# Seven landing buffers for weights become ten, in space taken from GpSimd's DMA descriptors

## The chip, the cores and the metric

The kernel runs on one core of a Trainium2 chip. The metric is device time in microseconds (us) of one execution. TensorE (PE in the profile, its weight loads PEld) multiplies matrices, VectorE (DVE) and ScalarE (ACT) work on elements, GpSimd (POOL) does some element work and issues small transfers, SyncE (SP) issues large transfers. 16 DMA engines carry every transfer, whoever issues it.

## The reference

One inference step of a hybrid model with two layers: 128 context tokens (group 0) and 128 latent tokens (group 1) of width 2048, which share the weights and differ in their modulation.

```
for l in range(2):
    shift1, scale1, gate1, shift2, scale2, gate2 = split(silu(c) @ w_mod[l] + b_mod[l])   # per group
    h = x * (1 + scale1) + shift1
    q, k, v, hq, hff, hfb, hi, hgt = split(h @ w_in[l])            # 2048 x 6656
    att = rms_norm(attention(q, k, v, sink))                       # 8 heads, 2 key/value heads
    hg, s_f, s_b = hgrn(hq, hff, hfb, hi, hgt, lower bounds, states)   # forward and backward scan
    x = layer_norm(alpha * x + gate1 * (concat(att, hg) @ w_o[l]))     # 2048 x 2048
    u = (x * (1 + scale2) + shift2) @ w_up[l]                      # 2048 x 8192
    x = layer_norm(alpha * x + gate2 * (square(relu(u)) @ w_down[l]))  # 8192 x 2048
```

Everything is float32. The outputs are x of both groups, keys and values of the context, and the final scan states.

## The kernel before, in words

All weights come from HBM once. A weight tile is 512 rows by 512 columns, 1 MB, and arrives as two halves of 128 partitions by 1024 floats (0.524 MB, 4 KB in each partition), each in a landing buffer `raw` of the pool `rawp`, which has `RAW_BUFS` = 7 buffers. `split` takes a half apart into a rounded high part `wh` (ScalarE, L1324) and the remainder `wl` (VectorE, L1325), each with a pool of `W_BUFS` = 4 halves. After `wl` the landing buffer is free. `mm_tile` then makes three products for each piece, high by high, high by low, and low by high, into accumulators in PSUM: lines L436, L438, L439 for units whose result is transposed, L448 to L450 for the others. Each unit (512 columns of a matrix) is four such tiles.

The modulation weights `w_mod` go through the same landing buffers. Part of them is multiplied on TensorE straight from the buffer (`Mod`, L203, and `ModQ`, L223, for the first two vectors of layer 0); part of them on VectorE (`ModH`, four L266 steps for each tile, the sum over partitions later on TensorE, L275). They are mixed in among the weight tiles in a list `seq` at set rates: in layer 0's projections 8/13, 16/13 and 1.2 modulation tiles for each weight tile, in layer 0's MLP 0.111 for TensorE and 0.45 for VectorE, in layer 1 far fewer. What a layer norm needs and has not come yet is put right ahead of it (`flush`).

The last part of the program walks through `seq`. `issue` puts the loads of up to 20 items ahead on SP's queue, in the order of `seq`, but stops when as many buffers are taken as `RAW_BUFS` says; `split` splits the current tile and the next weight tile; after every tile a few steps of side work (attention, the scans, modulation, layer norm outputs) are advanced by `pump`. The queues of SP and GpSimd are in the order in which the program writes them. ScalarE, VectorE and TensorE are ordered by the framework's planner, which works with estimated durations and the number of buffers in each pool; the orders are fixed when the kernel is built.

GpSimd issues the small loads (`side`): constants, residual rows `Y` (L1185), gate rows `G` (L876), bias rows, scan states, scale and shift of the layer norms (L951, L952, L998, L999). Descriptors of its transfers are written into a space reserved in each partition of SBUF, 16 KB unless `Bacc` is told otherwise (`dynamic_dma_scratch_size`). ScalarE issues the stores of states, keys and gate rows (`back`). SP and ScalarE write no descriptors into that space.

A unit's results are taken from PSUM by steps such as L1236 (accumulator `Z` of the MLP), L1240 and L1241 (gated sum), L887 to L892 (residual sum), L541 and L511 (softmax), L742 and L748 (scan).

```
                while len(hs) < 2:
                    if live[0] >= RAW_BUFS:
                        return
                    raw = rawp.tile([128, 1024], F32, tag="raw", name=nm("raw"))
                    nc.sync.dma_start(raw, half_src(it, len(hs)))
```

Of the kernel before, what the change touches and what calls it, by code (L numbers as in the profile page):

```python
# [22 lines left out]
SCALE = 128.0 ** -0.5  # L23
LN_EPS = 1e-5
RMS_EPS = 1e-6
RAW_BUFS = 7
W_BUFS = 4
PUMP2 = 2
PUMP = 3
# [16 lines left out]


class Unit:
    """One [2048, 512] block of a weight matrix against the tokens of both groups."""

    def __init__(self, kind, src, act, done, groups=range(4)):
        self.kind = kind
# [9 lines left out]
def tile_hybrid_step(ctx: ExitStack, tc: tile.TileContext, a, o):  # L62
    nc = tc.nc
    PS = bass.MemoryType.PSUM

    const = ctx.enter_context(tc.tile_pool(name="const", bufs=1))
    rawp = ctx.enter_context(tc.tile_pool(name="rawp", bufs=RAW_BUFS))
    whp = ctx.enter_context(tc.tile_pool(name="whp", bufs=W_BUFS))
# [18 lines left out]
    def u(tag, n=512):  # L87
        return up.tile([128, n], F32, tag=tag, name=nm(tag), bufs=BUFS[tag])

    def pair(s):  # L90
        t = actp.tile([128, 1024], F32, tag="a", name=nm(s))
        return [t[:, 0:512], t[:, 512:1024]]

    def small(n, s="s"):
        return sp.tile([128, 16], F32, tag="s", name=nm(s))[:, :n]

    def bank(s="b"):
        return sdp.tile([128, 512], F32, tag="sd", name=nm(s))

    def v3(t, n):  # L100
        return t.rearrange("p (m x) -> p m x", m=n)
# [3 lines left out]
    side = nc.gpsimd  # L105
# [4 lines left out]
        side.dma_start(t, a[name])  # L110
        return t

    # ---- constants and small parameters
    craw = const.tile([128, 16, 2], F32, name="craw")
    nc.sync.dma_start(craw, a["cT"])
    stat = const.tile([128, 16, 2], F32, name="stat")
# [25 lines left out]
    K = {}  # L142
# [37 lines left out]
        dve.tensor_tensor(lb1, m, e0, ALU.subtract)  # L180
        dve.tensor_scalar(oml1, lb1, -1.0, 1.0, ALU.mult, ALU.add)

    # ---- modulation vectors
    modT = {}
    grow = {}

    class Mod:
        """One modulation vector; its four blocks of 512 features lie 32 partitions apart."""

        def __init__(self, l, v):  # L190
            self.l, self.v = l, v
# [13 lines left out]
                          tile_position=(0, 32 * j))  # L205

    class ModQ:
        """512 features of one modulation vector, its products summed over four parts of the rows."""

        def __init__(self, l, v, q):  # L210
            self.l, self.v, self.q = l, v, q
# [33 lines left out]
    dve.memset(ones32, 1.0)  # L245

    class ModH:
        """1024 features of one modulation vector, summed over the rows on the vector engine, over partitions on the PE."""

        def __init__(self, l, v, h):  # L250
            self.l, self.v, self.h = l, v, h
# [103 lines left out]
                dve.tensor_tensor(mtv[:, j], ptv[:, j], bt[:, j], ALU.add)  # L355
        modT[l, v] = mt

    # ---- queue of side work, advanced one stage per weight tile
    tasks = deque()

    def start(gen, banks=0):
# [36 lines left out]
            pump(1)  # L398
        return dct[key]

    # ---- activations, transposed and split in two
    def new_act(s):
        return (actp.tile([128, 4, 256], F32R, tag="a", name=nm(s + "h")),
                actp.tile([128, 4, 256], F32R, tag="a", name=nm(s + "l")))
# [3 lines left out]
        act.copy(hi, src)  # L408
        dve.tensor_tensor(lo, src, hi.bitcast(F32), ALU.subtract)  # L409

    # ---- weight tiles
    class Main:
        def __init__(self, unit, kg):
            self.unit, self.kg = unit, kg
# [35 lines left out]
                        pe.matmul(ps, lhsT=lo[:, k, gs], rhs=wh[k], start=False, stop=e and k == 3)  # L450

    def ev(un, eng0, eng1, where):
        """The two blocks of a finished unit, in SBUF; what earlier parts of its rows gave is added."""
        if un.base is None:
            t = pair("ev") if where == "A" else [u(where), u(where)]
            eng0(t[0], un.ps[0])
            eng1(t[1], un.ps[1])
            return t
        for b in range(2):
            dve.tensor_tensor(un.base[b], un.ps[b], un.base[b], ALU.add)  # L460
        return un.base

    # ---- attention
    kS = {}
    kP = {}
    vP = {}
# [30 lines left out]
        kP[l], kS[l], vP[l], vS[l] = kt, ks, kvp, (kvs, vc)  # L497

    def softmax(l, j, banks_, nk, e):
        """e[t, head, key] = exp(scale * s - m); returns 1 / (sum + exp(K["sink"] - m))."""  # L500
        hb = 4 // len(banks_)
        mx, t, sm, es = small(4), small(4), small(4), small(4)
        for b, ps in enumerate(banks_):
            dve.tensor_reduce(mx[:, hb * b:hb * b + hb], v3(ps, hb), AX.X, ALU.max)
        sk = K["sink"][:, 8 * l + 4 * j:8 * l + 4 * j + 4]
        dve.scalar_tensor_tensor(mx, mx, SCALE, sk, ALU.mult, ALU.max)
        dve.tensor_tensor(es, sk, mx, ALU.subtract)
        dve.tensor_scalar(t, mx, -1.0, None, ALU.mult)
        for h in range(4):
            ps = v3(banks_[h // hb], hb)[:, h % hb]  # L510
            act.activation(e[h], ps, AF.Exp, scale=SCALE, bias=t[:, h:h + 1], accum_out=sm[:, h:h + 1])  # L511
        act.activation(es, es, AF.Exp)
        dve.tensor_tensor(sm, sm, es, ALU.add)
        dve.reciprocal(sm, sm)
        return sm
# [91 lines left out]
            tk[l, "att"] = start(att_fin(l), 1)  # L607

    def rstd_of(v, n, scale, eps):
        """(scale * v + eps) ** -0.5, refined by one Newton step."""  # L610
        x, r, t = small(n), small(n), small(n)
        dve.tensor_scalar(x, v, scale, eps, ALU.mult, ALU.add)
        act.activation(r, x, AF.Ln)
        act.activation(r, r, AF.Exp, scale=-0.5)
        dve.tensor_tensor(t, r, r, ALU.mult)
        dve.tensor_tensor(t, t, x, ALU.mult)
        dve.tensor_scalar(t, t, -0.5, 1.5, ALU.mult, ALU.add)
        dve.tensor_tensor(r, r, t, ALU.mult)
        return r
# [27 lines left out]
                split_act(hls[j], (slice(None), slice(0, 4), slice(128 * g, 128 * g + 128)), v3(t, 4))  # L647
            mix[l, j] = hls[j]

    # ---- HGRN  # L650
    vh = {}
    qh = {}
    oh = {}
# [210 lines left out]
            dve.scalar_tensor_tensor(lo, pt, gcol, hi.bitcast(F32), ALU.mult, ALU.subtract)  # L864
        mix[l, 2 + G] = hl_

    # ---- residual, layer norm
    xres = {}
    yt = {}
    bst = {}  # L870
# [8 lines left out]
    def stats(key, n, g):  # L879
        if n == 0:  # L880
            bst[key, g] = sp.tile([128, 24], F32, tag="bs", name=nm("bs"), bufs=4)
        dve.bn_stats(bst[key, g][:, 6 * n:6 * n + 6], yt[key, n, g])

    def add_gated(key, n, g, ps, gt, first, last):
        """y += gate * ps (y starts as alpha * residual)."""
        t = gt
        dve.tensor_tensor(t, ps, gt, ALU.mult)  # L887
        y = yt[key, n, g]
        if first:
            dve.scalar_tensor_tensor(y, y, ALPHA, t, ALU.mult, ALU.add)  # L890
        else:
            (dve if n == 3 else pool).tensor_tensor(y, y, t, ALU.add)  # L892
        if last:
            stats(key, n, g)

    def ln_stat(key):
        """Mean and 1 / sqrt(variance + eps) of every token, one column a group."""
        mv = small(4)
        for g in range(2):
            dve.bn_aggr(mv[:, 2 * g:2 * g + 2], bst[key, g])  # L900
        r = rstd_of(mv.rearrange("p (g x) -> p g x", g=2)[:, :, 1], 2, 1.0, LN_EPS)
        return [(mv[:, 2 * g:2 * g + 1], r[:, g:g + 1]) for g in range(2)]
# [17 lines left out]
        return A, B  # L920

    def ln_mod(key, AB, dst):
        """h = (xhat * g + b) * (1 + scale) + shift, transposed and split."""
        A, B = AB
        for n in range(4):
            hl = new_act("h")
            for g in range(2):
                y = yt[key, n, g]
                pt = bank("pt")
                for c in range(4):  # L930
                    pe.transpose(pt[:, 128 * c:128 * c + 128], y[:, 128 * c:128 * c + 128], K["ident"])
                t = u("ed")
                if g == 0:
                    dve.tensor_tensor(v3(t, 4), v3(pt, 4),
                                      A[:, 4 * n:4 * n + 4, g:g + 1].to_broadcast([128, 4, 128]), ALU.mult)
                    dve.tensor_tensor(v3(t, 4), v3(t, 4),
                                      B[:, 4 * n:4 * n + 4, g:g + 1].to_broadcast([128, 4, 128]), ALU.add)
                else:
                    for c in range(4):
                        act.activation(t[:, 128 * c:128 * c + 128], pt[:, 128 * c:128 * c + 128], AF.Identity,  # L940
                                       scale=A[:, 4 * n + c, g:g + 1], bias=B[:, 4 * n + c, g:g + 1])
                split_act(hl, (slice(None), slice(0, 4), slice(128 * g, 128 * g + 128)), v3(t, 4))
            dst[n] = hl
# [47 lines left out]
            store(n, g)  # L991

    def ln_out(key, li, sink_fn):
        """x = xhat * g + b, off the critical path."""
        tag = "G"
        for n in range(4):
            gt, bt = u(tag), u(tag)
            side.dma_start(gt, a["lng"][li:li + 1, 512 * n:512 * n + 512].partition_broadcast(128))  # L998
            side.dma_start(bt, a["lnb"][li:li + 1, 512 * n:512 * n + 512].partition_broadcast(128))  # L999
            for g in range(2):  # L1000
                y = yt.pop((key, n, g))
                pool.tensor_tensor(y, y, gt, ALU.mult)
                pool.tensor_tensor(y, y, bt, ALU.add)
                sink_fn(n, g, y)
            yield

    # ---- the program
    modseq = deque()
    poolseq = deque()
    POOLED = ((0, 5), (1, 0), (1, 1), (1, 2), (1, 5))  # L1010
# [271 lines left out]
    for l in range(L):  # L1282
        layer(l)

    # ---- emit
    raws = {}
    live = [0]
    nd = [0]
# [8 lines left out]
    def issue(upto):  # L1297
        while nd[0] < min(upto, len(seq)):
            it = seq[nd[0]]
            if it[0] in ("main", "mod"):  # L1300
                hs = raws.setdefault(nd[0], [])
# [3 lines that stand above are left out]
# [24 lines left out]
            nsplit[0] += 1  # L1329

    def main_ahead(i, n):
        """Index just past the n-th main tile after position i."""
        j = i + 1
        while j < len(seq) and n > 0:
            if seq[j][0] == "main":
                n -= 1
            j += 1
        return j

    for i, it in enumerate(seq):  # L1340
        issue(i + 1 + 20)
        split(i + 1)
        if it[0] == "main":
            split(main_ahead(i, SPLIT_AHEAD))
            issue(i + 1 + 20)
            m = it[1]
# [137 lines left out]
```

## Time and profile before

| | us |
|---|---|
| median of 3 runs | 2680.48 |
| lowest and highest | 2664.18, 2681.79 |
| profiled execution, first to last instruction | 2678.7 |
| TensorE busy in it | 2553.7 (95%) |
| VectorE, ScalarE, GpSimd busy | 1862.2, 1212.4, 226.2 |

The profiled span is 1.8 us below the median. Spans of matmuls overlap and their ends are modelled, so busy time on TensorE says when it had work and not how fast it went. The kernel reads 643.32 MB from HBM and writes 6.88 MB.

### The profile page before, as it was taken

What the parts mean: (1) busy time and instruction counts of PE and PEld (TensorE: products, weight loads), DVE (VectorE), ACT (ScalarE), POOL (GpSimd) and SP (SyncE); (2) the same over time, 40 slices, a digit from 0 to 9 for tenths busy, and PEclk for the clock granted to TensorE, in tenths of its full rate; (3) what the DMA queues carried; (4) which work ended last, traced back from release to release, by engine and by line L of the source; (5) the groups of instructions that cost most, each with busy time, mean ns of one, the idle gap of its engine ahead of it and who ended that gap; (6) DMA issues with size and microseconds to landing.
All of it is one profiled execution on the core that took longest, in us unless ns stands there. A gap on an engine that the chain in (4) does not pass through costs nothing.

```text
span 2678.7 us, 41129 instructions
## 1 busy us (share of the span) xinstructions
PE 2553.7 (95%) x16276; PEld 2189.5 (82%) x16276; DVE 1862.2 (70%) x2290; ACT 1212.4 (45%) x1655; POOL 226.2 (8%) x266
## 2 busy tenths in 40 slices
PE   7999999988999999999998999999899999999996
PEld 4787777656988978979876989898798898998985
DVE  3555777658877868787778777787876556566566
ACT  2434554334444534533533656544454444443442
POOL 2000000014100000000014100000330000000002
PEclk9999999999999999999999999999899999999998
DMA  9879878778887878787778656476666666666664
GB/s 325 272 270 316 279 245 273 264 246 322 276 285 268 276 251 298 267 274 249 260 260 275 238 172 228 149 237 200 200 213 221 208 212 229 203 219 211 212 207 141
DMA packets 192369, 652.91 MB, mean 244 GB/s; under 512 B 22752, under 2 KB 25376, under 8 KB 192176
## 3 DMA queue, kind: packets, MB, share of 16 engines
q1 hardware_dynamic: 177680, 614.56, 67.5%
q0 software_dynamic: 11552, 33.04, 4.2%
q8 instruction: 127, 2.08, 0.3%
q10 hardware_dynamic: 2944, 2.69, 0.3%
q14 instruction: 66, 0.54, 0.1%
HBM read 643.32 MB, written 6.88 MB: 243 GB/s over the span
## 4 chain that ended last, share of the span: by engine, by line
PE 60%; issue 24%; DMA 8%; DVE 6%; ACT 2%; POOL 0%; SPq 0%; DVEq 0%; ACTq 0%; POOLq 0%
PE acc L436 9%; PE acc L438 9%; PE acc L439 9%; PE acc L448 9%; PE acc L449 9%; PE acc L450 9%; DMA raw<-in_w_mod_dram 3%; DMA raw<-in_w_in_dram 2%; PE psm L203 2%; DMA raw<-in_w_o_dram 2%; DVE wl L1325 2%; PE pX L777 1%; ACT wh L1324 1%; PE psm L223 1%; DMA out_nsf_dram<-lf 1%
## 5 line engine op out<-in xcount | busy, mean ns | idle before, releaser
L1324 ACT CAST wh<-raw 128x1024 fp32r<-128x1024 f32 x784 | 821.6, 1050 | 1184.6 <-PE acc L450 444.2
L1325 DVE TENSOR_TENSOR wl<-raw,wh 128x1024 fp32r<-128x1024 f32 x784 | 973.2, 1249 | 455.6 <-ACT wh L1324 452.8
L436 PE MATMUL acc<-hh,wh 128*128 128x256 f32 x3072 | 880.0, 287 | 7.2 <-DVE Z L1236 2.6
L439 PE MATMUL acc<-hh,wl 128*128 128x256 f32 x3072 | 873.6, 285 | 13.2 <-DVE wl L1325 13.0
L438 PE MATMUL acc<-hl,wh 128*128 128x256 f32 x3072 | 873.4, 284 | 1.4 <-DVE hl L409 1.4
L436 PEld LDWEIGHTS acc<-hh,wh 128*128 128x128 f32 x3072 | 592.3, 193 | 45.3 <-issue 20.0
L439 PEld LDWEIGHTS acc<-hh,wl 128*128 128x128 f32 x3072 | 592.2, 193 | 15.3 <-DVE wl L1325 15.2
L438 PEld LDWEIGHTS acc<-hl,wh 128*128 128x128 f32 x3072 | 592.5, 193 | 3.0 <-DVE hl L409 2.3
L266 DVE SCALAR_TENSOR_TENSOR ma<-raw,stat,ma 128x1024 f32<-128x1024 f32 x300 | 381.8, 1293 | 136.8 <-DMA raw<-in_w_mod_dram 135.3
L448 PE MATMUL acc<-wh,fh 128*128 128x512 f32 x1024 | 401.3, 392 | 9.4 <-DVE Z L1236 8.0
L449 PE MATMUL acc<-wl,fh 128*128 128x512 f32 x1024 | 399.7, 390 | 1.8 <-DVE wl L1325 1.8
L450 PE MATMUL acc<-wh,fl 128*128 128x512 f32 x1024 | 399.0, 390 | 0.0
L448 PEld LDWEIGHTS acc<-wh,fh 128*128 128x128 f32 x1024 | 192.6, 188 | 60.1 <-DVE Z L1236 9.7
L449 PEld LDWEIGHTS acc<-wl,fh 128*128 128x128 f32 x1024 | 192.7, 188 | 43.0 <-DVE wl L1325 3.8
L450 PEld LDWEIGHTS acc<-wh,fl 128*128 128x128 f32 x1024 | 192.5, 188 | 40.3
L448 PE MATMUL acc<-wh,hh 128*128 128x512 f32 x320 | 131.1, 413 | 3.8 <-ACT hh L408 2.4
L449 PE MATMUL acc<-wl,hh 128*128 128x512 f32 x320 | 129.4, 404 | 2.4 <-DVE wl L1325 2.4
L450 PE MATMUL acc<-wh,hl 128*128 128x512 f32 x320 | 128.7, 403 | 1.6 <-DVE hl L409 1.6
L876 POOL DMA_DIRECT2D G<-gr x48 | 26.2, 546 | 968.0 <-DVE Z L1241 431.4
L203 PE MATMUL psm<-raw,stat 128*2 128x512 f32 x640 | 96.3, 599 | 9.8 <-DMA raw<-in_w_mod_dram 9.1
L448 PE MATMUL acc<-wh,mxh 128*128 128x512 f32 x256 | 103.4, 404 | 0.9 <-ACT mxh L408 0.5
L449 PE MATMUL acc<-wl,mxh 128*128 128x512 f32 x256 | 100.3, 393 | 0.8 <-DVE wl L1325 0.8
(366 smaller groups left out, 2133.0 us busy)
## 6 DMA issues: line engine op xcount, KB each, us to landing
raw<-in_w_mod_dram SPq DMA_DIRECT2D x384, 512.0 KB, 5.5
raw<-in_w_up_dram SPq DMA_DIRECT2D x256, 512.0 KB, 5.7
raw<-in_w_down_dram SPq DMA_DIRECT2D x256, 512.0 KB, 5.0
raw<-in_w_in_dram SPq DMA_DIRECT2D x208, 512.0 KB, 5.6
raw<-in_w_o_dram SPq DMA_DIRECT2D x64, 512.0 KB, 6.3
G<-gr POOLq DMA_DIRECT2D x48, 256.0 KB, 5.2
G<-in_lng_dram POOLq DMA_DIRECT2D x12, 256.0 KB, 5.3
G<-in_lnb_dram POOLq DMA_DIRECT2D x12, 256.0 KB, 6.1
```

The lines of the kernel that those rows point to most:

```text
L203: pe.matmul(self.ps[32 * j:32 * j + 2, :], lhsT=stat[:, k, :], rhs=raw[j // 2][:, 512 * (j % 2):512 * (j % 2) + 512], start=k == 0, stop=k ...
L223: pe.matmul(self.ps[32 * j:32 * j + 2, :], lhsT=stat[:, 4 * k + j, :], rhs=raw[j // 2][:, 512 * (j % 2):512 * (j % 2) + 512], start=k == 0 ...
L266: dve.scalar_tensor_tensor(self.acc[g], raw[h], c, self.acc[g], ALU.mult, ALU.add)
L436: pe.matmul(ps, lhsT=w0, rhs=hi[:, k], start=f and k == 0 and m % 2 == 0, stop=False, skip_group_check=True)
L438: pe.matmul(ps, lhsT=w0, rhs=lo[:, k], start=False, stop=False, skip_group_check=True)
L439: pe.matmul(ps, lhsT=w1, rhs=hi[:, k], start=False, stop=e and k == 3 and m % 2 == 1, skip_group_check=True)
L448: pe.matmul(ps, lhsT=hi[:, k, gs], rhs=wh[k], start=f and k == 0, stop=False)
L449: pe.matmul(ps, lhsT=hi[:, k, gs], rhs=wl[k], start=False, stop=False)
L450: pe.matmul(ps, lhsT=lo[:, k, gs], rhs=wh[k], start=False, stop=e and k == 3)
L777: pe.matmul(pX[:, 128 * m + 32 * c:128 * m + 32 * c + 32], lhsT=kd[:, 128 * m:128 * m + 128], rhs=qb[:, 128 * m + 32 * c:128 * m + 32 * c ...
L1324: act.copy(wh, r)
L1325: dve.tensor_tensor(wl, r, wh.bitcast(F32), ALU.subtract)
```

## The change

`RAW_BUFS` goes from 7 to 10, three more buffers of 4 KB in each partition. The program is built with `dynamic_dma_scratch_size=4096`, so that 4 KB of each partition hold GpSimd's descriptors, 12 KB less. The limit in `issue` follows `RAW_BUFS`, so loads are written up to ten halves ahead. The other lines of the diff remove comments and docstrings.

```diff
-RAW_BUFS = 7
+RAW_BUFS = 10
...
-    nc = bacc.Bacc("TRN2", target_bir_lowering=False, num_devices=1)
+    nc = bacc.Bacc("TRN2", target_bir_lowering=False, num_devices=1, dynamic_dma_scratch_size=4096)
```

## Rows read from the trace of the kernel before

**Rows 1.** The page: span and busy time of the engines (share, instructions).

```profile
span 2678.7 us, 41129 instructions
...
PE 2553.7 (95%) x16276; PEld 2189.5 (82%) x16276; DVE 1862.2 (70%) x2290; ACT 1212.4 (45%) x1655; POOL 226.2 (8%) x266
```

**Rows 2.** Stretches: start:end, length, busy us of each engine, PE clock, DMA share, GB/s.

```profile
0.00:67.00 67.00, 51.35 (x271) 28.40 (x272) 20.84 (x40) 19.41 (x31) 16.51 (x31) 0.95 0.93 325
67.00:603.00 536.00, 512.75 (x3336) 394.21 (x3336) 340.15 (x583) 229.57 (x383) 26.11 (x42) 0.99 0.80 271
603.00:670.00 67.00, 56.66 (x381) 41.79 (x378) 57.36 (x71) 31.44 (x50) 30.74 (x25) 1.00 0.90 323
670.00:1407.00 737.00, 714.00 (x4499) 629.61 (x4499) 570.24 (x528) 322.74 (x357) 25.10 (x27) 0.99 0.79 269
1407.00:1474.00 67.00, 59.80 (x299) 42.55 (x298) 55.70 (x62) 26.26 (x42) 26.79 (x27) 0.95 0.82 276
1474.00:1876.00 402.00, 388.78 (x2658) 353.48 (x2657) 311.36 (x527) 226.22 (x386) 26.15 (x40) 0.98 0.61 204
...
1943.00:2657.00 714.00, 713.99 (x4578) 651.23 (x4576) 433.82 (x391) 325.43 (x362) 41.51 (x45) 1.00 0.64 210
```

**Rows 3.** Waits of SP's queue, whole span: total us, times, longest.

```profile
SPq L1306 <- DVE wl L1325: 1497.9, 714, 22.1
```

**Rows 4.** DMA issues by line: count, size, median us to landing.

```profile
raw<-in_w_mod_dram SPq DMA_DIRECT2D x384, 512.0 KB, 5.5
```

**Rows 5.** Timeline of SP, 820 to 846 us: start, length of the merged piece.

```profile
823.14 2.66 SPq L1306 DMA_DIRECT2D raw<-in_w_mod_dram  x2
...
828.94 1.47 SPq L1306 DMA_DIRECT2D raw<-in_w_mod_dram  x2
839.70 5.05 SPq L1306 DMA_DIRECT2D raw<-in_w_up_dram  x4
```

**Rows 6.** Timeline of VectorE, 836 to 838 us; idle time before in brackets.

```profile
837.25 1.28 DVE L266 SCALAR_TENSOR_TENSOR ma<-raw,stat,ma 128x1024 f32<-128x1024 f32 x1 [7.20 <-DMA raw<-in_w_mod_dram]
```

**Rows 7.** Timeline of TensorE, 839.5 to 840 us.

```profile
839.72 0.58 PE L439 MATMUL acc<-hh,wl 128*128 128x256 f32 x1 [2.88 <-DVE wl L1325]
```

**Rows 8.** Waits of TensorE, 670 to 1407 us.

```profile
PE acc L439 <- DVE wl L1325: 9.1, 3, 3.4
PE acc L448 <- DVE Z L1236: 8.0, 3, 4.0
PE acc L436 <- DVE Z L1236: 2.6, 2, 1.9
```

**Rows 9.** Waits of VectorE, 670 to 1407 us.

```profile
DVE ma L266 <- DMA raw<-in_w_mod_dram: 96.0, 38, 7.2
```

**Rows 10.** Waits of TensorE, 67 to 603 us.

```profile
PE po L545 <- ACT e L541: 5.7, 1, 5.7
...
PE acc L436 <- ACT wh L1324: 1.7, 2, 1.1
PE acc L439 <- DVE wl L1325: 1.2, 2, 0.6
```

**Rows 11.** Timeline of ScalarE, 545 to 547 us.

```profile
545.94 1.04 ACT L1324 CAST wh<-raw 128x1024 fp32r<-128x1024 f32 x1 [5.41 <-DMA raw<-in_w_o_dram]
```

**Rows 12.** Waits of TensorE, 603 to 670 and 1407 to 1474 us.

```profile
PE psm L203 <- DMA raw<-in_w_mod_dram: 5.4, 5, 2.5
...
PE psm L203 <- DMA raw<-in_w_mod_dram: 3.7, 4, 2.8
```

**Rows 13.** Waits of SP's queue, 360 to 385 us.

```profile
SPq L1306 <- DMA out_nsb_dram<-lf: 2.2, 1, 2.2
```

**Rows 14.** DMA issues by line: count, size, median us to landing.

```profile
G<-gr POOLq DMA_DIRECT2D x48, 256.0 KB, 5.2
```

**Rows 15.** Timeline of GpSimd, 505 to 512 and 2620 to 2630 us.

```profile
508.01 0.54 POOL L876 DMA_DIRECT2D G<-gr  x1 [11.04 <-DVE Y L890]
...
2623.02 0.58 POOL L951 DMA_DIRECT2D w<-in_lng_dram  x1
```

## The prediction

> **What bounds the kernel now.** I read the page's totals first, then a table of stretches, then the waits in each stretch. TensorE is busy for 2553.7 of 2678.7 us [rows 1], so what is there to win is the rest: 125.0 us of idle time. The stretches show where it lies [rows 2]. Busy time subtracted from length, it is 15.7 us in the first 67 us, 23.3 us in the input and output projections of layer 0 (67 to 603), 10.3 us around its first layer norm, 23.0 us in its MLP (670 to 1407), 7.2 us around the next norm, 13.2 us in the projections of layer 1 (1474 to 1876), and nothing in the MLP of layer 1 (713.99 of 714.00 us busy); the remainder is layer 1's first norm and the tail after the last matmul. That last stretch is the measure for the others: the same code with the same seven landing buffers keeps TensorE full when the core takes in 210 GB/s. Where the kernel also streams the modulation weights (269 to 323 GB/s), TensorE has holes. VectorE and ScalarE are far from full in all stretches, so neither sets the end by its total.
>
> The queue that issues weight loads (SP) spends most of its time waiting for VectorE to release a landing buffer: 1497.9 us [rows 3]. That by itself costs nothing, since a full set of buffers is what one wants; a cost arises where a load that could go out waits for a buffer and is then missed. A load takes a median 5.5 us from issue to landing [rows 4].
>
> One such case shows the mechanism. In layer 0's MLP a pair of modulation loads goes out from 828.94 us [rows 5]; VectorE, whose instructions run in a fixed order, sits idle for 7.20 us until the first of the pair can be multiplied at 837.25 [rows 6]; the low half of the next weight tile stands behind it on VectorE, and TensorE stops for 2.88 us until 839.72 [rows 7]. In between SP had no free buffer.
>
> **The change, part by part.** Ten buffers in place of seven: a load waits for the buffer that came free three issues earlier. In the case above the third issue before 828.94 ended at 825.80 (823.14 plus 2.66) [rows 5], so the load goes out about 3.1 us earlier. I use 3.1 us as the lead for each late load; it leaves 4.1 us of VectorE's 7.20 us wait, and nothing of TensorE's 2.88, as TensorE was late by less than the lead.
>
> *Layer 0's MLP.* TensorE's waits with a late load ahead of them, or a VectorE step that stood in the queue behind one, are 9.1, 8.0 and 2.6 us, 19.7 us in eight waits [rows 8]; the longest are 3.4 and 4.0 us, so a lead of 3.1 us for each leaves 0.3 and 0.9, and 18.5 us could go. VectorE's 96.0 us of waiting for modulation loads in this stretch [rows 9] is the stock this comes from. I take 16, because the accumulator steps on Z also queue behind VectorE's own work (570.24 of 737 us busy [rows 2]), which no buffer shortens. Bounds: 0 and 19.7.
>
> *Layer 0's projections.* Of the 23.3 us, 5.7 us stand behind a softmax copy on ScalarE, 1.7 and 1.2 behind the two halves of a weight tile: 8.6 us [rows 10]. The 5.7 us come from a cast that waited 5.41 us for an output-projection load [rows 11], with the copy behind it on ScalarE; the lead takes 3.1 of them. With the other two that is 6.0, and I take 6. Bounds: 0 and 8.6; the remaining 14.7 us are waits between steps of attention and the recurrences, and I give nothing for them.
>
> *The two norms.* There the modulation vectors still missing are loaded in one burst, and TensorE waits 5.4 and 3.7 us for them [rows 12]. The transfer engines are at 0.90 and 0.82 of their time [rows 2], so a lead helps only as far as the burst starts sooner: three buffers of 0.524 MB at 323 GB/s are 4.9 us of transfer. That is about what each burst costs, and since part of the lead is itself lost to the full engines I take 3 for each, 6. Bounds: 0 and 9.1.
>
> *The rest.* In the first 67 us the engines are at 0.93 and 325 GB/s: the buffers can't speed what the transfers pace, 0 (bounds 0 and 3). Layer 1's projections stream 204 GB/s; I take 1 (bounds 0 and 13.2, its whole idle time). Layer 1's MLP has nothing to give: 0.
>
> *What the change adds.* SP waits for one thing more. A weight load waited 2.2 us for the landing of a store that ScalarE had issued from a tile it shares no byte with [rows 13]: the transfers of the two queues take turns on a small set of landing marks, and who takes a mark waits for its last owner. With loads going out three places earlier this happens somewhat more often; behind the waiting load on SP stand only further loads, and they have the new lead. I charge 1 us (bounds 0 and 6, three such waits). GpSimd's side transfers now share the engines with a deeper queue; its loads of gate rows take a median 5.2 us [rows 14], and they are issued well ahead, so 0 (bounds 0 and 4).
>
> *The smaller reserve.* GpSimd issues a load in 0.58 us, eight of them back to back from 2623.02 without an idle gap [rows 15]. By the 5.2 us of [rows 14] nearly all eight were in flight at once. So 16 KB hold about eight, and a quarter should hold at least two. What a wait for room would cost isn't in the trace; I take 0 and give the bad end to a rival.
>
> The sum: 16 + 6 + 6 + 1 - 1 = 28 us. From the profiled 2678.7 that is 2650.7; the median of the three runs is 1.8 us above the profiled span, so 2652.5 us, 1.04% below the 2680.48. Next to be late then are VectorE's own chains (scan and softmax steps) and the norms' arithmetic, which were there before. One of the three runs was 2664.18, 0.6% under the median, so about 1% is what a measurement of this kernel can tell from no change.
>
> **The rivals.** *B, the transfers themselves are the limit where they are dense.* For it: 0.80 and 0.79 of the engines' time in the two long stretches of layer 0, 0.90 in the flush. Against: in the flush they moved 323 GB/s, in the two long stretches 271 and 269 [rows 2], so a sixth more is possible; and SP issued nothing from 830.41 (828.94 plus 1.47) to 839.70 [rows 5], while VectorE waited for data. If it holds, half the MLP's 16 remains, 2 of the projections, none of the burst: 10 us, 2670. The Trainium skill (SBUF — State Buffer, A bandwidth-pool intuition that's wrong) says that HBM is nearly always the bottleneck end to end, at some 358 GB/s for a core. By that rule buffers add nothing wherever the core is near that rate; the trace agrees only for the first 67 us and the flush (325 and 323 GB/s), and in the MLP the row stands at 269.
>
> *C, one wait takes the place of another.* VectorE releases nearly all buffers [rows 3], in a fixed order that the framework's planner laid out, and it plans ScalarE, VectorE and TensorE anew with ten buffers. If lateness comes from that order, the loads land sooner and lie unused, and a new order may lose what the lead wins. Against: 96.0 us in which VectorE had nothing to do but wait for data [rows 9]. Gain 0, 2680, give or take 8. That the change doesn't do what it says is its other form: the marks of [rows 13] keep the seventh or eighth load back, so that the new buffers stay empty. Against: loads in flight rarely need more than a few places, as 5.5 us [rows 4] at 269 GB/s are under three loads.
>
> *D, slower: GpSimd waits for room in its descriptors.* If 4 KB held one load only, each would take 5.2 us in place of 0.54. In the output projection GpSimd issues batches of two gate and two residual loads, with 11.04 us idle before such a batch [rows 15]; four in series take 20.8 us against 11.04 + 2.2 between batches, 7.6 us late in each of four batches, 30 us, in each of two layers; and the eight loads at 2623.02 would end at 2664.6, after the end of the last matmuls at 2657 [rows 2], with the last gate loads behind them, some 17 us on the tail. Together 77 us, less the 28: 2729.5. With room for two, a batch takes 10.4 us and everything is hidden, so it decides between one and two in flight; the eight in a row speak against it. The Trainium skill (DMA: Bandwidth & Descriptors, SWDGE vs HWDGE vs iDMA) says that GpSimd's descriptors lie in rings in a part of SBUF set aside for them; no run here shows what GpSimd does when they are full.
>
> **How the numbers follow.** The forecast, gains of 18 to 45 us (2636 to 2663): 0.52, of which 0.37 above 1%. More, because VectorE's side chains also move up (down to 2620): 0.07. B: 0.18. C: 0.16. D: 0.07. Faster by over 1%: 0.37 + 0.07 = 0.44; slower: 0.07; within 1%: 0.49. The range from 2630 to 2686 leaves out D and half of the larger gains.
>
> **What the changed profile would show.** Right: VectorE's wait for modulation loads in layer 0's MLP falls from 96.0 to under 40 us; TensorE's waits there under 6 us; ScalarE's and VectorE's waits for loads down throughout layer 0, the transfer rate there up by 1 to 3%; layer 1's MLP unchanged. B: share of the engines above 0.9 and times to landing well above 5.5 us. C: VectorE waits for loads fall, TensorE's don't. D: idle time on GpSimd ahead of its load issues. The forecast is wrong above all if the waits counted under Z and the softmax copy are not the loads' doing.

## The result, and the profile after

The changed kernel takes 2643.29 us (median of 4 runs, 2641.68 to 2646.98) against 2679.14 us before (now four runs): a ratio of 0.9873, 95% interval 0.9848 to 0.9899. The profiled execution has a span of 2639.9 us. The forecast was 2652.5, so the gain is 36 us where 28 were summed.

The page of the changed kernel (span, busy time by engine, the chain that ended last, and the group of VectorE's multiply-and-add steps on the modulation weights with the idle time ahead of it):

```profile
span 2639.9 us, 41114 instructions
...
PE 2536.6 (96%) x16276; PEld 2178.1 (83%) x16276; DVE 1862.5 (71%) x2290; ACT 1214.5 (46%) x1655; POOL 230.9 (9%) x266
...
PE 76%; DMA 10%; DVE 9%; issue 3%; ACT 1%; SPq 0%; POOL 0%; DVEq 0%; ACTq 0%; POOLq 0%
...
L266 DVE SCALAR_TENSOR_TENSOR ma<-raw,stat,ma 128x1024 f32<-128x1024 f32 x300 | 388.5, 1313 | 113.4 <-DMA raw<-in_w_mod_dram 111.8
```

Beside [rows 1], TensorE has 103.3 us without work in place of 125.0, and it is busy for 17.1 us less with the same 16276 instructions; its mean granted clock is 0.988 in place of 0.982. Loads are still a tenth of the chain, and VectorE still waits 111.8 us for modulation weights (135.3 before).

To see where the time went I cut both traces at the same places in the program: the last matmul of line 233, then the first transposes of each layer norm (line 931) on TensorE, which end the projections of layer 0, its MLP and the projections of layer 1; the last cut is the last matmul. Columns as in [rows 2]. The kernel before:

```profile
0.00:227.00 227.00, 206.95 (x1330) 151.71 (x1331) 104.17 (x137) 77.74 (x100) 16.51 (x31) 0.98 0.85 292
227.00:630.00 403.00, 376.91 (x2367) 281.12 (x2367) 275.34 (x523) 176.77 (x320) 31.71 (x48) 0.99 0.79 270
630.00:1432.00 802.00, 772.18 (x4883) 673.72 (x4882) 629.43 (x590) 353.28 (x405) 52.66 (x48) 0.99 0.80 273
1432.00:1926.00 494.00, 469.82 (x3046) 418.38 (x3045) 386.09 (x606) 267.84 (x443) 63.42 (x80) 0.98 0.65 213
1926.00:2657.00 731.00, 727.78 (x4656) 664.61 (x4656) 450.75 (x412) 334.27 (x382) 53.76 (x54) 0.99 0.63 207
```

The changed kernel:

```profile
0.00:222.00 222.00, 205.41 (x1335) 152.22 (x1336) 108.39 (x142) 81.04 (x103) 16.56 (x31) 0.97 0.89 311
222.00:618.00 396.00, 376.76 (x2373) 280.61 (x2371) 271.15 (x520) 175.63 (x318) 31.77 (x48) 0.99 0.80 273
618.00:1400.00 782.00, 764.00 (x4880) 668.07 (x4878) 627.68 (x588) 353.75 (x405) 54.88 (x48) 1.00 0.81 278
1400.00:1887.00 487.00, 464.13 (x3039) 413.76 (x3038) 386.48 (x607) 267.35 (x443) 65.77 (x80) 0.99 0.65 219
1887.00:2618.00 731.00, 726.13 (x4656) 663.45 (x4656) 452.27 (x411) 334.22 (x382) 53.84 (x54) 1.00 0.62 204
```

Five stages went from 227, 403, 802, 494 and 731 us to 222, 396, 782, 487 and 731: 5, 7, 20 and 7 us shorter, and nothing in layer 1's MLP. By these two traces half the gain is in layer 0's MLP, as forecast (how far one stage of one trace can be trusted, the first experiment shows). The transfer rate in layer 0's two stages is up by 1 and 2% and layer 1's MLP is unchanged, as I had named; but in layer 0's MLP the main sign fails. The waits of VectorE and of TensorE in that stage of the changed kernel (total, times, longest):

```profile
DVE ma L266 <- DMA raw<-in_w_mod_dram: 77.0, 32, 5.2
...
PE acc L448 <- DVE Z L1236: 6.8, 3, 2.4
PE acc L439 <- DVE wl L1325: 5.1, 6, 1.4
```

VectorE's wait was to fall from 96.0 [rows 9] to under 40, TensorE's behind it from 19.7 [rows 8] to under 6; they stand at 77.0 and 11.9. Three more buffers, and modulation loads are late nearly as often (32 times, 38 before). Whether the buffers are worth so little, or something takes back what they give, is what the experiments had to tell. The suspect: the framework's planner, which fixes the order of VectorE's, ScalarE's and TensorE's instructions when the kernel is built, planned anew for ten buffers. Counted in the two traces, the 300 multiply-and-add steps of line 266 stand on VectorE 2.07 weight halves (line 1325) earlier on average than before.

### The profile page after: what moved, and what is told of

The parts are those of the page before. It is cut to its first block, busy times and chain, and to the rows that moved or that the text cites. A ratio compares the mean times of both kernels' runs of the same rounds, so it can differ in the third digit from the quotient of the medians.

```text
span 2639.9 us, 41114 instructions
## 1 busy us (share of the span) xinstructions
PE 2536.6 (96%) x16276; PEld 2178.1 (83%) x16276; DVE 1862.5 (71%) x2290; ACT 1214.5 (46%) x1655; POOL 230.9 (9%) x266
## 4 chain that ended last, share of the span: by engine, by line
PE 76%; DMA 10%; DVE 9%; issue 3%; ACT 1%; SPq 0%; POOL 0%; DVEq 0%; ACTq 0%; POOLq 0%
PE acc L436 12%; PE acc L439 12%; PE acc L438 12%; PE acc L448 11%; PE acc L449 11%; PE acc L450 11%; DMA raw<-in_w_mod_dram 6%; DVE wl L1325 3%; DVE ma L266 2%; PE psm L203 2%; PE pX L777 1%; DMA raw<-in_w_up_dram 1%; DMA raw<-in_w_in_dram 1%; PE psm L223 1%; DMA out_nsf_dram<-lf 1%
## 5 line engine op out<-in xcount | busy, mean ns | idle before, releaser
L266 DVE SCALAR_TENSOR_TENSOR ma<-raw,stat,ma 128x1024 f32<-128x1024 f32 x300 | 388.5, 1313 | 113.4 <-DMA raw<-in_w_mod_dram 111.8
L450 PE MATMUL acc<-wh,mxl 128*128 128x512 f32 x256 | 101.5, 398 | 0.0
```

The costliest lines, as they stand in the source:

```text
L266: dve.scalar_tensor_tensor(self.acc[g], raw[h], c, self.acc[g], ALU.mult, ALU.add)
```

## The experiments

Each ratio is to the kernel before on the same chip, with its 95% interval. Each edit is shown against the changed kernel, by its main lines; stored orders, and what was done to them, stand in words. In the kernels whose order is held, a stored list of each engine's instructions is laid over the program as edges of the kind that adds no wait (`NoSync`):

```diff
     with tile.TileContext(nc) as tc:
         tile_hybrid_step(tc, a, o)
+        fix_order(tc)
...
+def fix_order(tc):
...
+        order = [mine[k] for k in np.cumsum(steps.astype(np.int64))]
+        for x, y in zip(order, order[1:]):
+            tc.add_manual_dep(y, x.name, mybir.DependencyInfo(
+                mybir.DependencyClass.NoSync, mybir.DependencyReason.DATA), reason="order")
```

The kernel before with its own order laid over it was not run. That the edges by themselves don't make a kernel fast is seen from two kernels that have them and take 2639.55 and 2769.56 us (below).

**The smaller reserve alone.**

```diff
-RAW_BUFS = 10
+RAW_BUFS = 7
```

> Seven buffers, 4 KB of descriptors: the reserve alone. The orders of all engines are those of the kernel before. Theory (late loads, depth): 2679 us, within 5 of the kernel before. Rival (GpSimd waits for room): slower by 15 us or more, with idle time on GpSimd ahead of its loads. Rival (the reserve or the new addresses bring the gain): 2650 or less.

2678.19 us, ratio 0.9992 [0.9980, 1.0004]. Taking 12 KB from GpSimd's descriptors neither costs nor gains anything that can be measured here. Rival D is out at this size, and what the change did came with the buffers.

The trace of this kernel also shows how far one stage of one trace can be trusted. Orders and number of buffers are those of the kernel before, yet layer 0's projections come out 10 us longer and its MLP 8 us shorter:

```profile
230.00:643.00 413.00, 385.10 (x2364) 284.53 (x2364) 276.36 (x524) 176.59 (x320) 31.75 (x48) 0.96 0.78 264
643.00:1437.00 794.00, 769.51 (x4885) 671.58 (x4885) 626.83 (x588) 353.37 (x405) 53.88 (x48) 0.99 0.81 276
```

Against this trace the changed kernel gains 17 us in the projections and 12 in the MLP, not 7 and 20. So a difference of some 10 us in one stage says little by itself.

**Ten buffers, order of the kernel before.**

```diff
+PLAN = {...}  # the order of the kernel before, on VectorE, ScalarE and TensorE
```

> Ten buffers, but ScalarE, VectorE and TensorE run their instructions in exactly the order of the kernel before. Theory (depth): most of the gain stays, 25 us or more of the measured 36: 2643 to 2654 us. Rival (the planner's new order brought it): 2672 to 2682. In between both share it in that proportion.

2601.19 us, ratio 0.9705 [0.9692, 0.9719]: faster than any number I had named. The buffers alone are worth 77 us, and the new order gives some 42 of them back (2643.29 less 2601.19). Its stages:

```profile
0.00:219.00 219.00, 202.83 (x1331) 151.31 (x1332) 104.26 (x138) 78.20 (x100) 16.51 (x31) 0.98 0.90 310
219.00:593.00 374.00, 368.14 (x2365) 278.25 (x2365) 272.25 (x519) 175.78 (x320) 31.69 (x48) 1.00 0.84 288
593.00:1357.00 764.00, 757.80 (x4882) 666.56 (x4879) 631.28 (x588) 353.32 (x405) 57.86 (x48) 1.00 0.83 286
1357.00:1845.00 488.00, 468.49 (x3046) 418.99 (x3046) 387.06 (x615) 268.18 (x443) 68.27 (x80) 0.98 0.67 220
1845.00:2575.00 730.00, 726.81 (x4656) 663.71 (x4656) 455.54 (x412) 334.10 (x382) 54.20 (x54) 1.00 0.63 205
```

Layer 0's MLP is 38 us shorter than before, its projections 29. In the MLP TensorE idles for 6.2 us (764.00 less 757.80) where it idled for 29.8, and its busy time is 14.4 us less with the same instructions, to one. What VectorE waits for ahead of line 266, over the whole span, shows no load any more, only these four short waits for ScalarE's first product:

```profile
L266 DVE SCALAR_TENSOR_TENSOR ma<-raw,stat,ma x300: 1262/1279/2333, 617.8 to 2471.3; 128x1024 f32<-128x1024 f32 x150
...
  ACT ma L264: 1.4, 4
```

**Eight and nine buffers, each planned for its own number.**

```diff
-RAW_BUFS = 10
+RAW_BUFS = 8    # and 9
```

> Eight buffers, the planner's own order for them. Theory: each buffer buys a lead of about 1 us for a late load, and the waits are up to 4 us long, so the first buffers bring most: 2660 to 2668 us. Rival (order): no rule in the number of buffers, anywhere from 2640 to 2690.

> Nine buffers, the planner's own order for them. Theory: between eight and ten, 2649 to 2658 us. Rival (order): no rule in the number of buffers, anywhere from 2640 to 2690.

2661.02 us, 0.9927 [0.9911, 0.9944], and 2660.81 us, 0.9924 [0.9901, 0.9946]. The ninth buffer adds nothing that can be measured, and nine came out above what I had expected. Counted as above, the steps of line 266 stand 0.75 and 1.42 weight halves earlier in their traces than in the kernel before; with ten it was 2.07. Each buffer is worth about 0.7 of a weight half to the planner.

**Only these steps moved, both ways.** First the old order with line 266 placed as in the ten-buffer plan, then the ten-buffer plan with line 266 placed as before:

```diff
-PLAN["DVE"] = order of before
+PLAN["DVE"] = order of before, steps of L266 after as many L1325 as in the new plan
...
-PLAN["DVE"] = new plan
+PLAN["DVE"] = new plan, steps of L266 after as many L1325 as in the order of before
```

> Ten buffers, the order of the kernel before on every engine, but VectorE's multiply-and-add steps on the modulation weights (line 266) stand where the ten-buffer plan puts them, about two weight halves earlier. Theory 1, these steps eat the lead of the new buffers: layer 0's MLP goes from the 764 us of the ten-buffer kernel in the old order to about 782, the projections, which hold hardly any such step, stay near 374, and the whole is 2619 to 2626 us. Rival, it is the other moved steps (weight halves against softmax and scan steps): 2601 to 2606 us.

> The reverse: ten buffers and the ten-buffer plan's own order, but the multiply-and-add steps on the modulation weights are put back where the order of the kernel before has them. Theory 1: layer 0's MLP near 765 us, the projections near 397, the whole 2618 to 2625. Rival, the other moved steps: within 5 us of the changed kernel, 2638 to 2648.

2639.55 us, 0.9851 [0.9837, 0.9866], and 2619.14 us, 0.9773 [0.9752, 0.9794]. Moving these 300 steps costs 38 us in the old order, more than I had expected (the end was to be 2619 to 2626), and putting them back gains 24 in the new one. Layer 0's MLP, and VectorE's wait for modulation loads in it, with the steps early:

```profile
595.00:1380.00 785.00, 766.15 (x4882) 668.24 (x4879) 626.18 (x588) 353.28 (x405) 57.12 (x48) 0.99 0.80 278
...
DVE ma L266 <- DMA raw<-in_w_mod_dram: 78.1, 31, 5.4
```

and the same stage of the new plan with the steps put back, with all that VectorE waits for ahead of line 266:

```profile
617.00:1387.00 770.00, 760.69 (x4883) 667.53 (x4880) 631.12 (x588) 353.54 (x405) 52.75 (x48) 1.00 0.83 284
...
  ACT ma L264: 1.2, 3
```

785 against 764 us, and 770 against 782: in the MLP the place of these steps explains the whole difference one way and two thirds of it the other. The 78.1 us are the 77.0 of the changed kernel over again, with everything else in the old order. The projections of layer 0 go with the other steps instead: 375 us in the first kernel (374 in the old order), 395 in the second (396 in the new one). So the 42 us have two parts, and they don't add up exactly (38 and, from 2601 to 2619, 18).

**One buffer more than the order was planned for.** Eight buffers in the order for seven, and ten in the order for nine:

```diff
+RAW_BUFS = 8,  PLAN = the order planned for seven
...
+RAW_BUFS = 10, PLAN = the order planned for nine
```

> Eight buffers in the order that was planned for seven. Theory 1, what counts is by how many buffers the kernel has more than its order was planned for: one spare buffer, so about a third of the 77 us that three gave, 2645 us (2625 to 2655), and about the same as ten buffers in the order planned for nine. Rival 2, the order for seven is simply a good one and any depth above it does: 2601 to 2615.

> Ten buffers in the order that was planned for nine. Theory 1: one spare buffer, 2625 to 2645 us, within 10 us of eight buffers in the order for seven. Rival 2, the order for seven is a good one and the order for nine is not: 2650 to 2665, as with its own nine buffers (2660.8).

2612.53 us, 0.9753 [0.9738, 0.9767], and 2610.70 us, 0.9747 [0.9731, 0.9764]. They are equal, as the theory wanted, and both far better than it had sized: one spare buffer brings most of the gain. VectorE's wait for modulation loads in layer 0's MLP, the first and the second kernel:

```profile
DVE ma L266 <- DMA raw<-in_w_mod_dram: 23.8, 17, 4.3
```

```profile
DVE ma L266 <- DMA raw<-in_w_mod_dram: 15.0, 17, 2.0
```

The first alone would have fitted the rival (2601 to 2615). That the order for seven is merely a lucky one falls with the second: the order for nine, which takes 2660.8 us with nine buffers, takes 2610.7 with ten.

**A floor under these steps, in a few lines.** No stored order; the planner plans for ten buffers, but may not move a step of line 266 ahead of the weight half emitted five before it:

```diff
+LAG = 5
...
+                        x = dve.scalar_tensor_tensor(self.acc[g], raw[h], c, self.acc[g], ALU.mult, ALU.add)
+                        if len(lows) >= LAG:
+                            tc.add_manual_dep(x.ins, lows[-LAG].ins.name, mybir.DependencyInfo(
+                                mybir.DependencyClass.NoSync, mybir.DependencyReason.DATA), reason="order")
...
+                    lows.append(dve.tensor_tensor(wl, r, wh.bitcast(F32), ALU.subtract))
```

> Ten buffers and a plan of the planner's own, with no recorded order: only each multiply-and-add step on the modulation weights may not pass the weight half that was emitted five halves before it. In the order that comes out these steps stand on average one weight half later than in the kernel before, three later than in the changed kernel; everything else is planned for ten buffers. Theory 1: VectorE's wait for the modulation loads falls from 111.8 us to under 30, layer 0's MLP from 782 to 762-770, the projections stay at 390-400, the whole is 2612 to 2625. Rival, steps that come later only release their buffers later and the other loads pay for it: 2635 to 2650.

2623.15 us, 0.9797 [0.9777, 0.9817], inside the range named. Over the whole span VectorE's wait ahead of these steps (now line 268) for modulation loads is gone:

```profile
  DMA raw<-in_w_mod_dram: 0.3, 2
```

Cut as above, layer 0's MLP takes 768 us and its projections 394: the one is repaired, the other not.

**One buffer fewer than planned, and four more.**

```diff
+RAW_BUFS = 9,  PLAN = the order planned for ten
...
+RAW_BUFS = 10, PLAN = the order planned for six
...
+RAW_BUFS = 11, PLAN = the order planned for seven, dynamic_dma_scratch_size=1024
-    sp = ctx.enter_context(tc.tile_pool(name="sp", bufs=24))
+    sp = ctx.enter_context(tc.tile_pool(name="sp", bufs=15))
```

> Nine buffers in the order that was planned for ten: one buffer fewer than planned. Theory 1: one buffer above the plan was worth 66 us at seven and 50 at nine, so one below it costs at least as much: 2690 to 2720, slower than the kernel before, with VectorE's wait for modulation loads well above 112 us. Rival, only the order counts and not its depth: 2643 to 2660.

> Ten buffers in the order that was planned for six: four buffers above the plan. Theory 1: one spare buffer gave 2611-2613, three gave 2601, so four give 2595 to 2605. Rival, the order for seven is a good one by itself: this one does worse, 2612 to 2640.

> Eleven buffers in the order planned for seven; the fourth spare buffer's room comes from GpSimd's reserve (1 KB in place of 4) and from the pool of small scratch tiles (15 in place of 24). Theory 1: 2595 to 2603. Rival D of the prediction at a smaller size, a reserve of 1 KB makes GpSimd wait for room: idle time ahead of its load issues, and 2620 or more.

2769.56 us, 1.0346 [1.0321, 1.0371]; 2607.33 us, 0.9738 [0.9715, 0.9762]; 2603.56 us, 0.9725 [0.9705, 0.9745]. One buffer too few for the order costs 126 us against the changed kernel, more than expected (the end was to be 2690 to 2720). In its layer 0 MLP:

```profile
DVE ma L266 <- DMA raw<-in_w_mod_dram: 135.0, 43, 6.9
...
PE acc L439 <- DVE wl L1325: 19.5, 13, 4.4
PE acc L448 <- DVE Z L1236: 11.0, 3, 5.0
PE acc L449 <- DVE wl L1325: 11.0, 9, 2.2
```

Four spare buffers bring nothing over three; 2607.33 lies between the ranges named for the theory (to 2605) and its rival (from 2612), 2603.56 at the theory's upper end (2603). All pairs of order and buffers together; they were timed on several chips, on which the kernel before took 2674 to 2679 us, and the ratios allow for that:

| order planned for | buffers | spare | us | ratio to before |
|---|---|---|---|---|
| 10 | 9 | -1 | 2769.6 | 1.0346 |
| 7 | 7 | 0 | 2679.1 | 1 |
| 8 | 8 | 0 | 2661.0 | 0.9927 |
| 9 | 9 | 0 | 2660.8 | 0.9924 |
| 10 | 10 | 0 | 2643.3 | 0.9873 |
| 7 | 8 | 1 | 2612.5 | 0.9753 |
| 9 | 10 | 1 | 2610.7 | 0.9747 |
| 7 | 10 | 3 | 2601.2 | 0.9705 |
| 6 | 10 | 4 | 2607.3 | 0.9738 |
| 7 | 11 | 4 | 2603.6 | 0.9725 |

Three more buffers with a plan of their own bring 36 us. One spare buffer brings 67 and 50 us in the orders for seven and nine, and 48 and 33 at the same eight and ten buffers; two more spare ones bring some 10, and then it ends. The fastest kernel measured is ten buffers in the order planned for seven; eleven in that order can't be told from it.

The traces of all fourteen kernels agree on layer 0's MLP. Cut as above, it takes 763 to 770 us in the seven in which VectorE's wait there for modulation loads is at most 24 us, 782 to 802 in the six in which it is 77 to 96, and 834 in the one with a buffer too few, where it is 135.

## Why the prediction was right, and where it wasn't

*The mechanism* (a load issued late for want of a buffer stops VectorE, and TensorE behind it) was right: more buffers in one and the same order take those waits away, and VectorE's steps moved earlier bring them back.

*The total* came out 9 us from the forecast as the difference of two effects that I had not sized: 77 us from the buffers and 42 lost to the new order. That it came so near is luck. Rival C named that loss ("a new order may lose what the lead wins") and set it against the whole gain as an either-or; it belonged in the sum as a term. My argument against C, the 96.0 us in which VectorE only waited for data, was no argument: orders planned to the last buffer keep such waits at seven, eight, nine and ten buffers (135.3, 124.4, 126.3 and 111.8 us over the whole span).

*Layer 0's MLP*, 16 us (bounds 0 and 19.7): 20 us in the changed kernel for the stage as cut above (12 against the first experiment's trace), which takes in parts of both norms; 38 with the old order (30), above the upper bound even with both norms' 9.1. The step that failed is taking TensorE's idle time for all there is to win. 23.6 of the 38 us were idle time, 14.4 were in its busy time.

Much of the 14.4 is the clock. In the kernel before, five stops of TensorE in this stage, 1.87 to 4.00 us long and all waits of the kinds in [rows 8], each have a stretch at a granted clock of 0.50 (1.2 GHz) towards their end or just behind; with one at the second norm that is 22.6 us in six stretches. The one at the stop of [rows 7], and the time behind it (columns as in [rows 2]):

```profile
839.30:842.70 3.40, 2.98 (x14) 2.98 (x15) 3.40 (x4) 0.00 (x0) 0.00 (x0) 0.50 0.48 149
842.70:852.00 9.30, 9.30 (x78) 8.30 (x78) 5.19 (x6) 4.20 (x4) 0.00 (x0) 1.00 0.93 308
```

With ten buffers in the old order one such stretch is left, at the first norm:

```profile
599.40:602.80 3.40, 3.40 (x14) 1.36 (x13) 3.40 (x5) 2.08 (x5) 2.38 (x3) 0.50 1.03 411
```

At 0.50 a matmul took 213 ns (14 in 2.98 us), at 1.00 it took 119 (78 in 9.30). By that, 19.2 us less at the lower clock are worth some 8 of the 14.4 us, an estimate; the rest was not traced.

*Layer 0's projections*, 6 us, and the *first norm*, 3: 7 us together in the changed kernel, 29 with the old order (17 and 39 against the first experiment's trace). Of the cases in which ScalarE waits for a weight load I had counted one, the cast of [rows 11]. ScalarE's waits for loads in this stage, before and with ten buffers in the old order (total, times, longest):

```profile
ACT wh L1324 <- DMA raw<-in_w_in_dram: 61.7, 25, 6.5
ACT wh L1324 <- DMA raw<-in_w_o_dram: 53.7, 16, 6.7
```

```profile
ACT wh L1324 <- DMA raw<-in_w_in_dram: 9.9, 5, 3.2
ACT wh L1324 <- DMA raw<-in_w_o_dram: 7.8, 3, 5.0
```

115 us in 41 waits became 18 in 8. But these waits don't explain the 29 us. The ten-buffer plan with line 266 put back has them just as short, and its stage takes 395 us:

```profile
ACT wh L1324 <- DMA raw<-in_w_o_dram: 8.8, 4, 4.9
ACT wh L1324 <- DMA raw<-in_w_in_dram: 7.8, 6, 3.7
```

TensorE's idle time in the stage is 26.1 us before, 5.9 with the old order and 19.2 in the changed kernel, so part of the 14.7 us for which I had given nothing ("waits between steps of attention and the recurrences") could be won too. Through which waits stays open.

*The two norms*, 6 us: TensorE's waits for the two bursts went from 9.1 us to 5.0, and to 0.5 with the old order.

*The first 67 us*, 0 because "the transfers pace" them: wrong. The same stretch, with seven buffers and the small reserve, and in the changed kernel:

```profile
0.00:67.00 67.00, 50.87 (x274) 28.63 (x275) 21.62 (x41) 20.17 (x31) 16.52 (x31) 0.90 0.93 325
```

```profile
0.00:67.00 67.00, 52.03 (x284) 30.65 (x285) 24.00 (x43) 21.66 (x33) 16.56 (x31) 0.92 1.00 360
```

A share of 0.93 was not full; it was an average, with 0.68 and 234 GB/s from 60 to 70 us in the kernel before, where the changed one has 1.03 and 397. The first stage took 227 and 230 us with seven buffers, 222 in the changed kernel and 219 with the old order. The Trainium skill (SBUF — State Buffer, A bandwidth-pool intuition that's wrong) puts a core's rate from HBM at some 358 GB/s. The trace agrees for these 67 us as a whole, but not on a limit: from 600 to 630 us the changed kernel moves 380 GB/s, at a share of 1.02.

*Layer 1's projections*, 1 us (bounds 0 and 13.2): 7 us, with the norms' share. *Layer 1's MLP*, 0: held, 731 us both times. *SP's extra waits*, 1 us: its waits for the landing of ScalarE's stores are 7.1 us in three in the changed kernel (2.2 in one before), 1.5 in one with the old order; what they cost the end was not measured.

*B*, transfers as the limit: refuted. Layer 0's two stages moved 270 and 273 GB/s before, 273 and 278 after, 288 and 286 in the old order with the same ten buffers.

*C's other form*, marks that keep the new buffers empty: does not hold. SP's waits for the landing of loads fell from 129 us to 105, and to 29 with the old order, in which the buffers bring 77 us.

*D*, GpSimd short of room: refuted at 4 KB by the first experiment, and its mechanism shown at 1 KB (below).

What stays open: why the planner moves these steps up with each buffer. That it counts on loads landing sooner than they do would fit, but no run tried it. Nor was the loss in layer 0's projections, some 20 us that go with the other moved steps, traced to single ones: ScalarE's waits for loads, the first guess, are not it.

## What to carry to other kernels

Where a planner orders the engines, a deeper buffer is two changes: hold the old order and time the buffer alone. Here planning for fewer buffers than the kernel has was worth more than the buffers with a plan of their own: one buffer over the plan is slack for loads that land late, and the plan must not be able to spend it. TensorE's idle time is no upper bound for what late operands cost: in these traces stops were followed by stretches at half the clock, which count as busy time. And a transfer share of 0.93 over a stretch can be an average of full and half idle ones. Lengths of stages from single traces differ by some 10 us between kernels of the same order and depth.

## What the runs showed of the hardware

GpSimd does wait for room in its descriptors, at a size that can be seen. With a reserve of 4 KB (the kernel of the first experiment) six loads of activations, each in 512 pieces (128 partitions, four runs of 512 bytes), go out in a row in 4.5 us; start and length, merged by twos:

```profile
42.79 1.50 POOL L138 DMA_DIRECT2D e<-in_xT_dram  x2
44.28 1.50 POOL L138 DMA_DIRECT2D ed<-in_xT_dram  x2
45.77 1.49 POOL L138 DMA_DIRECT2D Z<-in_xT_dram  x2
47.24 0.55 POOL L110 DMA_DIRECT2D ident<-in_ident_dram  x1
```

With 1 KB (eleven buffers) they go out one by one, with 4.27 to 6.64 us between them in which GpSimd waits for nothing that the trace can name (idle time in brackets):

```profile
43.35 0.76 POOL L138 DMA_DIRECT2D e<-in_xT_dram  x1
49.73 0.77 POOL L138 DMA_DIRECT2D e<-in_xT_dram  x1 [5.63 <-issue]
54.77 0.75 POOL L138 DMA_DIRECT2D ed<-in_xT_dram  x1 [4.27 <-issue]
...
76.92 0.55 POOL L110 DMA_DIRECT2D ident<-in_ident_dram  x1
```

The six take 33.6 us (43.35 to 76.92) in place of 4.5. The loads of gate rows and norm parameters, in 128 pieces of 2 KB, still go out in twos and eights at 1 KB. The end was hardly later for it, if at all (2603.6 us with eleven buffers, 2601.2 with ten and 4 KB). Both kinds of load are 256 KB, so in these runs the room goes by pieces, not by loads or bytes, and D's wait begins somewhere between 4 and 1 KB for this kernel. That eight loads went out in a row [rows 15] told little of it, since those were of the kind with few pieces. The kernel with 1 KB also has one more landing buffer and fewer small tiles; these loads use neither.
